# One decoder layer on one core: the first head's loads, the end of the out-projection and the block ring's places are rearranged

## The chip, the cores and the metric

One core of a Trainium2 chip runs the whole layer in one launch. The metric is the device time in microseconds. A few executions of a kernel are timed and the median is given; one more execution is recorded by the hardware profiler, and its page and trace are what the rows below come from.

## What is computed

Batch 1, 512 tokens behind 16 learned meta tokens (528 positions), width 2048, one layer, everything in fp32:

```python
h = concatenate([meta, x])                       # 528 x 2048
p = rmsnorm(h, g_mix) @ w_in                     # 2048 x 6144: q, k, v, b, c, u of 1024 columns each
o_attn = stick_breaking_attention(rmsnorm(q), rmsnorm(k), v)    # 8 heads of 128
o_conv = b * causal_dwconv3(c * u)                              # 1024 channels
h = h + concatenate([rmsnorm(o_attn), rmsnorm(o_conv)]) @ w_out
n2 = rmsnorm(h, g_ffn)
h = h + (silu(n2 @ w_gate) * (n2 @ w_up)) @ w_down              # 5632 inner columns
return h[16:]
```

Nearly all the work is in the products with w_in, w_out, w_gate, w_up and w_down.

## The kernel before

Activations lie transposed: 16 tiles of 128 channels by 528 (later 512) positions. Each fp32 operand is used as a sum of two parts, hi (rounded to the format fp32r) and lo (what is left), and a product is three matmuls: hi·hi, hi·lo, lo·hi.

**The weight stream.** All weights come in one fixed order, the list `loads`, on SyncE's DMA queue (SP) into four places of `w_buf`, each 128 partitions by 1024 columns. For each weight, ScalarE (ACT) casts it into hi (L189) and VectorE (DVE) subtracts to get lo (L190), into one of three slots of `s_buf`. `next_w` keeps two to three splits ahead of TensorE (PE), and when a place has been used for the last time, `done_with` issues the next load into it, so a load waits for VectorE's split. Every engine runs its instructions in the order in which they were put down; a scheduler sets that order when the program is built, with priorities, and it does not change at run time.

**Pairs.** The conv group (from its third channel tile on), the FFN's gate and up products (44 pairs) and the down product use products of 2x2 blocks in seven block products instead of eight: `pair_product` takes the blocks in the order 0 to 6 (the first pair of a kind begins with block 5), and VectorE adds weight quadrants for it (L198, L215). The blocks of the activations are formed once, stored in DRAM, and loaded again.

**Stages.** First head (k and q products side by side while x arrives, then v and the attention), seven more heads, the conv group, the out-projection (w_out), the FFN's 44 pairs, the down product. The places that the change and the prediction touch:

- *The first head* (L362 to L388). For each of five groups of k tiles (2, 2, 4, 4, 4): load x tiles (`load_x`, L341, also on SyncE), cast nh (L348 on ScalarE, L350 on GpSimd for the odd tiles from the fourth on), nl on VectorE (L351), one step of the k and of the q product, squares (L356, L359) and their adds (L360). The names in the trace: pk, pq, pv are the three products' accumulators, ssx the sum of squares over all channels (L330), which gives x's norm. Small vectors (gains) come in `vec` (L72).
- *The out-projection's end* (L887 to L970, called "the seam" in the prediction). For 16 output tiles, the attention half (acts `oa`) and the conv half (acts `oc`) of the product go to two halves of an accumulator `po`. The residual then takes four VectorE or GpSimd steps (L902 to L905), a scaling, and splits into the FFN's blocks f. Blocks 3, 4 and 6 go through DRAM (`fx`), since there is no room for them until the out-projection's buffers are released: the six loads f<-fx (L952, on GpSimd's queue) stand behind the last tile. `h_scale` is the norm of the FFN's input, a chain of small operations on all positions.
- *The ring* (L1028 to L1103). The down product takes its 22 k tiles in chunks of 4, 6, 6 and 6. Each chunk needs seven blocks of activations, loaded from DRAM (ring<-fd, L1042, on GpSimd's queue) into twelve ring places; chunk 0's blocks 1 to 6 lie in buffers of their own, `first`, and its block 0 in ring place 0. Places 1, 3, 4, 5 share memory with `first` and open when chunk 0 is done. `out_T<-d` (L1071) are the stores that add results to the output.

```python
    groups = {0: (0, 1), 1: (1, 2), 3: (1, 1), 4: (1, 1), 5: (1, 1), 6: (2, 1), 7: (2, 5)}
    def ring_place():
        n_ring[0] += 1
        return ring[(n_ring[0] - 1) % 12]
```

In `groups`, `i: (p, m)` says that m places from number i on lie in buffer p.

Of the kernel before, what the change touches and what calls it, by code (L numbers as in the profile page):

```python
# [15 lines left out]
P = 128  # L16
D = 2048
# [16 lines left out]
def hybrid_layer(ctx: ExitStack, tc: tile.TileContext, xT, w_in, w_out, w_gu, w_down, vecs, out):  # L34
# [37 lines left out]
    gp.dma_start(vec, vecs)  # L72
# [21 lines left out]
    carry = const.tile([P, P], F32R, name="carry")  # L94
    ve.tensor_copy(carry, later)
    ve.tensor_copy(carry[0:1, :], ones[0:1, :])
    ones_r = keep.tile([P, P], F32R, name="ones_r")
    ve.tensor_copy(ones_r, ones)
    later_r = const.tile([P, P], F32R, name="later_r")
    ve.tensor_copy(later_r, later)  # L100
# [44 lines left out]
    for i, b in ((0, 1), (1, 1), (0, 0), (1, 0), *((i, b) for i in range(2, KT) for b in range(2))):  # L145
        plan_raw(w_out[OUT_TILES[i], b], 8)
# [10 lines left out]

    quads, sums, split_w, used, loaded = {}, {}, [], [0], [0]
# [8 lines left out]

    def load_at(place):
        key, n, w = loads[loaded[0]]
        loaded[0] += 1  # L170
        t = w_buf[:, place : place + n * P]
        quads[key] = t, place, n
        nc.sync.dma_start(t.rearrange("p (t c) -> p t c", t=2) if len(w.shape) == 3 else t, w)

    def done_with(key):
        _, place, n = quads[key]
        if loaded[0] < len(loads):
# [126 lines left out]
    def square_sum(acc, src, first, s=None):  # L304
        if first:
            sc.activation(acc, src, AF.Square)
        else:
            s = t512(src.shape[-1], "r", 3)[:, : src.shape[-1]] if s is None else s
            sc.activation(s, src, AF.Square)
            gp.tensor_tensor(acc, acc, s, ALU.add)  # L310
# [32 lines left out]
    def split_x(k):  # L343
# [3 lines left out]
        if k < 4 or k % 2 == 0:  # L347
            sc.activation(nh, xts[k], AF.Copy, scale=g)  # L348
        else:
            gp.tensor_scalar(nh, xts[k], g, 0.0, ALU.mult, ALU.add)  # L350
# [17 lines left out]
    load_at(PLACES[0])  # L368
    load_x(0)
    load_at(PLACES[1])  # L370
    for a, b in FIRST:
        for k in range(len(xts), b):
            load_x(k)
        if not a:
            load_at(PLACES[2])
            load_at(PLACES[3])
        for k in range(a, b):
            split_x(k)
        if b == KT:
            for k in range(a, b):  # L380
                square_x(k)
            after(8, x_scale)
        for step in steps:
            next(step)
        if b < KT:
            for k in range(a, b):
                square_x(k)
# [86 lines left out]
    def head(h):  # L474
# [9 lines left out]
        after(8, qk_norm(halves(pk, H), g_k, L, kn[:, :L], (kh, kl, 384), f"k{h}"))  # L484
# [9 lines left out]
        after(9 if h else 10, qk_norm(pq[:, 0, :], gq_s, SEQ, qn, (qh, ql, SEQ), f"q{h}"))  # L494
# [125 lines left out]
    for h in range(HEADS):  # L620
        if h:
            after(6, lambda h=h: form_blocks(h - 1))
# [44 lines left out]
    for j in range(CONV_FIRST):  # L667
        if j == 0:
            after(2, lambda: form_blocks(7))
# [113 lines left out]
    for j in range(CONV_FIRST, HEADS, 2):  # L783
# [19 lines left out]
        for m in range(2):  # L803
            s = t512(SEQ, "e", 2)[:, :SEQ] if j == HEADS - 2 else cpool.tile([P, SEQ], F32, tag="s", name=f"sq{j}_{m}")
            conv_out(j + m, gbs[m][:, META - C0 :], ys[m], slots[m][:, 0], slots[m][:, 1], s, ve)
# [79 lines left out]
    for i in range(2):  # L885
        run(wide_product(ps_out[i][:, 0, :], oa))
    for i, j in enumerate(OUT_TILES):  # L887
        hj = wide_tmp("h", bufs=2)
        gp.dma_start(hj, xT[j][:, META:])
        if 0 < i < KT - 1:  # L890
            ps = new_ps()
            run(wide_product(ps[:, 0, :], oa))
            run(wide_product(ps[:, 1, :], oc))
        ps = ps_out[i]
        t1, t2 = wide_tmp("t1"), wide_tmp("t2")
        half, k = divmod(j, 8)
# [4 lines left out]
        def residual(eng):  # L901
            ve.tensor_tensor(t1, ps[:, 0, :], acc_a, ALU.mult)  # L902
            eng.tensor_tensor(hj, hj, t1, ALU.add)
# [16 lines left out]
        if i == KT - 1:  # L920
            with tc.high_priority(1 << 20):
                residual(ve)
                square_sum(acc_h, hj, False, wide_tmp("s"))
                mixed_blocks()
            oapool.release()
# [7 lines left out]
            rings, n_ring, ring = {}, [7], {}  # L933
# [16 lines left out]
            for s, n in ((3, 7), (4, 7), (6, 8)):  # L950
                for part in range(2):
                    gp.dma_start(acts[s][:, part, :n], fx[s][:, part, :n], max_dma_last_dim=4096)  # L952
            split_f(3, 6)
            split_f(4, 7)
        else:
# [244 lines left out]
```

## Time and profile before

| | us |
|---|---|
| median of 3 executions | 2069.37 (2069.09 to 2069.38) |
| the profiled execution | 2071.88 |
| its span on the core | 2069.7 |
| TensorE busy in the span | 2038.4 (98%) |
| VectorE / ScalarE / GpSimd busy | 1724.3 / 1046.4 / 412.3 |
| mean granted TensorE clock | 0.994 |

How to read the rows: a group row gives the busy time, the number of instructions and the mean length; a timeline row gives the start in the span, the length, the engine, the kernel's line, the operation, and in brackets how long the engine stood idle before and what released it. Rows of a wait list give the total, the number and the longest. The rows of stretches give the busy time of each engine in a window, then the TensorE clock that was granted (1.00 is full speed), the DMA engines' busy share and what they moved. SPq is SyncE's queue, PEld are TensorE's weight loads.

### The profile page before, as it was taken

How to read it: one execution, taken by the hardware profiler on the slowest of the kernel's cores; microseconds unless marked ns; L12 is line 12 of the kernel's file. 1: busy time of each engine (PE TensorE's matmuls, PEld its weight loads, DVE VectorE, ACT ScalarE, POOL GpSimd, SP SyncE). 2: the span in 40 equal slices, each digit the busy share in tenths (PEclk: the TensorE clock that was granted, in tenths of full speed). 3: DMA queues.
4: the chain of work that ended last, by engine and by line, in shares of the span. 5: the costliest groups of instructions: out<-in, count | busy, mean ns of one | idle time of the engine just before them, and what ended most of it. 6: DMA issues, size and time to landing. Idle time of an engine off the chain costs nothing.

```text
span 2069.7 us, 39728 instructions
## 1 busy us (share of the span) xinstructions
PE 2038.4 (98%) x16158; PEld 1972.2 (95%) x16158; DVE 1724.3 (83%) x2186; ACT 1046.4 (51%) x1511; POOL 412.3 (20%) x559
## 2 busy tenths in 40 slices
PE   7999999999999998999999999999999999999999
PEld 6999999999998887999999999999999999999999
DVE  7878877578877677898998998998999987888887
ACT  5666666444443434455555545555554543444443
POOL 4111111220014444111011011111111252223110
PEclk9999999999999999999999999999999999999999
DMA  6343334563356656556465565565555999989864
GB/s 207 106 152 123 113 123 136 206 172 103 102 195 192 186 169 222 159 160 184 148 173 159 148 173 148 151 172 158 155 167 158 284 308 266 252 241 248 238 155 87
DMA packets 161687, 362.21 MB, mean 175 GB/s; under 512 B 13457, under 2 KB 73361, under 8 KB 161505
## 3 DMA queue, kind: packets, MB, share of 16 engines
q1 hardware_dynamic: 78368, 225.80, 34.7%
q0 software_dynamic: 83136, 133.89, 24.5%
q8 instruction: 126, 2.06, 0.4%
q14 instruction: 57, 0.46, 0.1%
HBM read 278.76 MB, written 80.87 MB: 174 GB/s over the span
## 4 chain that ended last, share of the span: by engine, by line
PE 92%; DVE 3%; DMA 1%; ACT 1%; issue 1%; POOL 0%; SPq 0%; DVEq 0%; ACTq 0%; POOLq 0%
PE x L732 13%; PE x L734 13%; PE x L733 13%; PE z L732 6%; PE z L733 6%; PE z L734 6%; PE y L733 3%; PE y L732 3%; PE y L734 3%; PE po L831 3%; PE po L833 3%; PE po L832 3%; PE pv L276 1%; PE pv L278 1%; PE pv L280 1%; PE pk L278 1%
## 5 line engine op out<-in xcount | busy, mean ns | idle before, releaser
L189 ACT CAST s_buf<-w_buf 128x1024 fp32r<-128x1024 f32 (+2 forms) x665 | 659.5, 992 | 789.9 <-PE x L733 360.5
L190 DVE TENSOR_TENSOR s_buf<-w_buf,s_buf 128x1024 fp32r<-128x1024 f32 (+2 forms) x665 | 769.8, 1158 | 186.4 <-ACT s_buf L189 185.5
L734 PE MATMUL x<-f,s_buf 128*128 128x256 f32 x1408 | 388.8, 276 | 6.2 <-DVE s_buf L190 6.2
L733 PE MATMUL x<-f,s_buf 128*128 128x256 f32 x1408 | 388.6, 276 | 1.3 <-DVE f L291 1.3
L732 PE MATMUL x<-f,s_buf 128*128 128x256 f32 x1408 | 388.6, 276 | 0.2 <-ACT f L290 0.2
L198 DVE TENSOR_TENSOR w_buf<-w_buf 128x1024 f32<-128x1024 f32 (+1 forms) x243 | 278.6, 1146 | 18.9 <-DMA w_buf<-w_in 10.1
L734 PEld LDWEIGHTS x<-f,s_buf 128*128 128x128 f32 x1408 | 265.7, 189 | 6.4 <-DVE s_buf L190 6.4
L733 PEld LDWEIGHTS x<-f,s_buf 128*128 128x128 f32 x1408 | 265.6, 189 | 1.5 <-DVE f L291 1.5
L732 PEld LDWEIGHTS x<-f,s_buf 128*128 128x128 f32 x1408 | 265.7, 189 | 0.5 <-ACT f L290 0.4
L1004 POOL DMA_DIRECT2D fd<-s x147 | 103.7, 923 | 694.5 <-DVE s L291 692.9
L734 PE MATMUL z<-f,s_buf 128*128 128x256 f32 x704 | 193.6, 275 | 0.0
L733 PE MATMUL z<-f,s_buf 128*128 128x256 f32 x704 | 193.6, 275 | 0.0
L732 PE MATMUL z<-f,s_buf 128*128 128x256 f32 x704 | 193.6, 275 | 0.0
L732 PE MATMUL x<-ring,s_buf 128*128 128x256 f32 x608 | 168.5, 278 | 3.9 <-DVE d L1085 3.9
L734 PE MATMUL x<-ring,s_buf 128*128 128x256 f32 x608 | 168.3, 277 | 0.7 <-DVE s_buf L190 0.7
L733 PE MATMUL x<-ring,s_buf 128*128 128x256 f32 x608 | 168.3, 277 | 0.0
L733 PEld LDWEIGHTS z<-f,s_buf 128*128 128x128 f32 x704 | 132.2, 188 | 0.1
L732 PEld LDWEIGHTS z<-f,s_buf 128*128 128x128 f32 x704 | 132.2, 188 | 0.0
L734 PEld LDWEIGHTS z<-f,s_buf 128*128 128x128 f32 x704 | 132.2, 188 | 0.0
L1071 POOL DMA_DIRECT2D out_T<-d x62 | 59.5, 989 | 308.5 <-DVE d L1079 241.7
L732 PEld LDWEIGHTS x<-ring,s_buf 128*128 128x128 f32 x608 | 115.4, 190 | 4.1 <-DVE d L1085 4.1
L734 PEld LDWEIGHTS x<-ring,s_buf 128*128 128x128 f32 x608 | 115.3, 190 | 0.9 <-DVE s_buf L190 0.9
(380 smaller groups left out, 5285.8 us busy)
## 6 DMA issues: line engine op xcount, KB each, us to landing
w_buf<-w_gu SPq DMA_DIRECT2D x176, 512.0 KB, 3.5
w_buf<-w_in SPq DMA_DIRECT2D x92, 512.0 KB, 3.4
fd<-s POOLq DMA_DIRECT2D x147, 256.0 KB, 5.3
w_buf<-w_down SPq DMA_DIRECT2D x96, 384.0 KB, 4.9
ring<-fd POOLq DMA_DIRECT2D x42, 768.0 KB, 9.2
w_buf<-w_out SPq DMA_DIRECT2D x32, 512.0 KB, 3.4
out_T<-d POOLq DMA_DIRECT2D x62, 256.0 KB, 5.5
fc<-st SPq DMA_DIRECT2D x8, 1040.0 KB, 6.2
```

Of the source, the lines that this page charges most:

```text
L189: sc.copy(hi, src)
L190: ve.tensor_tensor(lo, src, hi.bitcast(F32), ALU.subtract)
L198: ve.tensor_tensor(sums[name], a, b, ALU.add)
L278: pe.matmul(ps, wh, al[:, a:b], start=False, stop=False)
L732: pe.matmul(p, hi[:, kk], act(0, k), start=start and j == k == 0, stop=False, skip_group_check=skip)
L733: pe.matmul(p, hi[:, kk], act(1, k), start=False, stop=False, skip_group_check=skip)
L734: pe.matmul(p, lo[:, kk], act(0, k), start=False, stop=k == n - 1, skip_group_check=skip)
L831: pe.matmul(ps, hi[:, kk], ah, start=k == order[0], stop=False)
L832: pe.matmul(ps, hi[:, kk], al, start=False, stop=False)
L833: pe.matmul(ps, lo[:, kk], ah, start=False, stop=k == order[-1])
L1004: gp.dma_start(fd[c][s][:, :, k], t[:, :, i])
L1071: gp.dma_start(two(out[j]), c, accum_op=ALU.add)
```

## The change

Three parts and a small one.

**A, the first head.** `vec` is loaded by SyncE ahead of everything. The first group's loads don't share four places: each of the ten head weights and v's first two get a place of their own in `w_buf` (`HEAD_PLACES`), and their end doesn't trigger a load (`EARLY`). All of these and the 16 x tiles are issued at the start. All x casts are on ScalarE and all adds of squares on VectorE, after the products; `x_scale` and the first head's norms are called two to three k tiles later. `form_blocks` (blocks of x for the conv group) is called one head later.

SyncE's queue at the start, before (xt are x tiles, w_buf weights; in brackets the semaphores that an instruction waits for, DMAHW of an earlier transfer, DVE of VectorE):

```order
L173 DMA w_buf<-w_in 128x256
L341 DMA xt_132<-xT 128x528
L173 DMA w_buf<-w_in 128x256
L341 DMA xt_135<-xT 128x528
L173 DMA w_buf<-w_in 128x256
L173 DMA w_buf<-w_in 128x512 [waits DMAHW0_49,DVE_49]
L173 DMA w_buf<-w_in 128x256
L341 DMA xt_179<-xT 128x528
L173 DMA w_buf<-w_in 128x512 [waits DMAHW2_49,DVE_49]
L341 DMA xt_181<-xT 128x528 [waits DMAHW1_49]
L173 DMA w_buf<-w_in 128x512 [waits DMAHW4_49,DVE_49]
```

and now:

```order
L72 DMA vec<-vecs 128x75
L172 DMA w_buf<-w_in 128x256
L340 DMA xt_127<-xT 128x528
L172 DMA w_buf<-w_in 128x256
L340 DMA xt_130<-xT 128x528
L172 DMA w_buf<-w_in 128x256
L340 DMA xt_133<-xT 128x528
L172 DMA w_buf<-w_in 128x256
L340 DMA xt_136<-xT 128x528 [waits DMAHW0_49]
L172 DMA w_buf<-w_in 128x512 [waits DMAHW1_49]
L340 DMA xt_139<-xT 128x528 [waits DMAHW2_49]
L340 DMA xt_141<-xT 128x528 [waits DMAHW3_49]
```

The waits for VectorE are gone from these rows; each transfer from the ninth on waits for the one eight before it.

**B, the out-projection's end.** The last two tiles go attention 14, attention 15, conv 14, conv 15 instead of tile by tile, and the attention half of the residual is a step of its own (`attention_half`). The last k tile of block 6 is split in place, so no block has more than seven k tiles to load from `fx`, and the loads come in the order 6, 3, 4. The last tiles' adds, `h_scale` (without its high priority) and the last tile's square add run on VectorE, and the last two output stores on SyncE.

GpSimd's queue there, before (f<-fx are the loads of blocks, acc_h and the work tiles belong to the norm):

```order
L970 DMA out_T<-w_7816 128x512
L310 TENSOR_TENSOR acc_h<-acc_h,w_7887 128x512
L961 DMA fx_6638<-st_7883 256x1x256
L952 DMA f_7929<-fx_6636 128x2x896 x2
L310 TENSOR_TENSOR acc_h<-acc_h,w_7900 128x512
L952 DMA f_7929<-fx_6637 128x2x896 x2
L952 DMA f_7930<-fx_6638 128x2x1024
L291 TENSOR_TENSOR work_r<-acc_h,work_r 128x512
L952 DMA f_7930<-fx_6638 128x2x1024
L299 TENSOR_TENSOR work_b<-work_a 128x512
```

and now:

```order
L985 DMA out_T<-w_7761 128x512
L309 TENSOR_TENSOR acc_h<-acc_h,w_7785 128x512
L892 DMA w_7822<-xT 128x512
L982 DMA fx_6636<-st_7780 256x1x256
L982 DMA fx_6637<-st_7780 256x1x256
L965 DMA f_7926<-fx_6638 128x2x896 x2
L965 DMA f_7925<-fx_6636 128x2x896 x2
L965 DMA f_7925<-fx_6637 128x2x896 x2
L1019 DMA fd_0_7952<-s_2_8205 256x1x256
```

The six loads stand in one row, with no operation of GpSimd between or behind them.

**C, the ring.** The ring starts at place 6 instead of 7, so that chunk 1 uses places 6 to 11 and then 0. Its sixth block is loaded with the fifth, in the last group of chunk 0, and its seventh in the middle of that group, as soon as place 0 (chunk 0's block 0) is free.

GpSimd's queue at the end of chunk 0, before (fd_5 and fd_6 are chunk 1's sixth and seventh block):

```order
L1042 DMA ring_17474<-fd_4_7965 128x2x768
L1042 DMA ring_7925<-fd_5_7966 128x2x768
L1071 DMA out_T<-d 256x1x256 x2
L1042 DMA ring_7925<-fd_5_7966 128x2x768
L1071 DMA out_T<-d_17446 256x1x256 x4
L1042 DMA ring_18326<-fd_6_7967 128x2x768 x2
L1071 DMA out_T<-d 128x512
```

and now:

```order
L1057 DMA ring_17472<-fd_4_7963 128x2x768
L1057 DMA ring_17472<-fd_5_7964 128x2x768
L1086 DMA out_T<-d 256x1x256 x2
L1057 DMA ring_17472<-fd_5_7964 128x2x768
L1057 DMA ring_7921<-fd_6_7965 128x2x768 x2
L1086 DMA out_T<-d_17444 256x1x256 x4
L1086 DMA out_T<-d 128x512
```

The seventh block's load has moved ahead of four output stores.

**D, the out-projection's start.** Its first two products go over the conv tiles in two parts; the parts are of four and four tiles instead of six and two. The last pair of conv outputs is put down at high priority.

The diff's core:

```diff
-    gp.dma_start(vec, vecs)
+    nc.sync.dma_start(vec, vecs)
...
+    EARLY = {loads[i][0]: i for i in range(2 * len(FIRST) + 2)}
+    HEAD_PLACES = [sum(2 * (b - a) * P for a, b in FIRST[:i]) + m * (b - a) * P for i, (a, b) in enumerate(FIRST) for m in range(2)]
+    HEAD_PLACES += [4096, 5120]
...
-        if loaded[0] < len(loads):
+        if key not in EARLY and loaded[0] < len(loads):
...
-        if k < 4 or k % 2 == 0:
-            sc.activation(nh, xts[k], AF.Copy, scale=g)
-        else:
-            gp.tensor_scalar(nh, xts[k], g, 0.0, ALU.mult, ALU.add)
+        sc.activation(nh, xts[k], AF.Copy, scale=g)
...
-            (gp, ve)[k % 2].tensor_tensor(accs[k % 2], accs[k % 2], s, ALU.add)
+            ve.tensor_tensor(accs[k % 2], accs[k % 2], s, ALU.add)
...
+    for i, (a, b) in enumerate(FIRST):
+        for m in range(2):
+            load_at(HEAD_PLACES[2 * i + m])
+            for k in range(len(xts), (a + b) // 2 if m == 0 else b):
+                load_x(k)
+    for place in HEAD_PLACES[2 * len(FIRST) :]:
+        load_at(place)
...
+            for place in PLACES:
+                load_at(place)
...
+    for k in range(KT):
+        square_x(k)
+    after(10, x_scale)
...
-        after(8, qk_norm(halves(pk, H), g_k, L, kn[:, :L], (kh, kl, 384), f"k{h}"))
+        after(8 if h else 11, qk_norm(halves(pk, H), g_k, L, kn[:, :L], (kh, kl, 384), f"k{h}"))
...
-        after(9 if h else 10, qk_norm(pq[:, 0, :], gq_s, SEQ, qn, (qh, ql, SEQ), f"q{h}"))
+        after(9 if h else 12, qk_norm(pq[:, 0, :], gq_s, SEQ, qn, (qh, ql, SEQ), f"q{h}"))
...
-        if h:
-            after(6, lambda h=h: form_blocks(h - 1))
+        if h > 1:
+            after(6, lambda h=h: form_blocks(h - 2))
...
-            for k in order[part * 6 : part * 6 + 6] if parts > 1 else order:
+            for k in order[part * 4 : part * 4 + 4] if parts > 1 else order:
...
+    def attention_half(i, eng):
+        hj, t1 = wide_tmp("h", bufs=2), wide_tmp("t1")
+        gp.dma_start(hj, xT[OUT_TILES[i]][:, META:])
+        ve.tensor_tensor(t1, ps_out[i][:, 0, :], acc_a, ALU.mult)
+        eng.tensor_tensor(hj, hj, t1, ALU.add)
+        return hj
...
+        elif i == KT - 2:
+            hs = [attention_half(m, ve) for m in (i, i + 1)]
+        if i >= KT - 2:
+            hj = hs[i - KT]
+            run(wide_product(ps_out[i][:, 1, :], oc))
...
-            for s, n in ((3, 7), (4, 7), (6, 8)):
+            for s in (6, 3, 4):
                 for part in range(2):
-                    gp.dma_start(acts[s][:, part, :n], fx[s][:, part, :n], max_dma_last_dim=4096)
+                    gp.dma_start(acts[s][:, part, :7], fx[s][:, part, :7], max_dma_last_dim=4096)
             split_f(3, 6)
             split_f(4, 7)
+            split_f(6, 3)
...
-            token_scale(acc_h, acc_h, D, "h", (w[:, 0], w[:, 1], a[:, 0], a[:, 1], b), gp)
+            token_scale(acc_h, acc_h, D, "h", (w[:, 0], w[:, 1], a[:, 0], a[:, 1], b))
...
-            rings, n_ring, ring = {}, [7], {}
+            rings, n_ring, ring = {}, [6], {}
...
-        for s in ((0, 1), (2, 3), (4,))[j - 1] if j else ():
+        for s in ((0, 1), (2, 3), (4, 5))[j - 1] if j else ():
...
+            (lambda: load_acts(1, 6)) if j == KT // 4 - 1 else None, lambda: second_sums(4 * j, c2, 2),
...
-            for s in (5, 6):
-                load_acts(1, s)
```

More of the change, by code (lines that the diff above doesn't have):

```diff
@@ L367, in hybrid_layer @@
     ]
-    load_at(PLACES[0])
-    load_x(0)
-    load_at(PLACES[1])
-    for a, b in FIRST:
[L372 to L376, printed above, removed]
+    for i, (a, b) in enumerate(FIRST):
[5 more added lines that the diff above has]
+        load_at(place)
+    limit[0] = 2 * len(FIRST)
+    for a, b in FIRST:
         for k in range(a, b):
@@ L379, in hybrid_layer @@
         if b == KT:
-            for k in range(a, b):
-                square_x(k)
-            after(8, x_scale)
+            for place in PLACES:
+                load_at(place)
+            limit[0] = len(ents)
         for step in steps:
             next(step)
-        if b < KT:
-            for k in range(a, b):
-                square_x(k)
+    for k in range(KT):
+        square_x(k)
+    after(10, x_scale)
+    later_r = const.tile([P, P], F32R, name="later_r")
+    ve.tensor_copy(later_r, later)
+    carry = const.tile([P, P], F32R, name="carry")
+    ve.tensor_copy(carry, later)
+    ve.tensor_copy(carry[0:1, :], ones[0:1, :])
     xpool.release()
@@ L968, in hybrid_layer @@
         if i < KT - 1:
-            square_sum(acc_h, hj, i == 0, wide_tmp("s"))
-        (gp if i < KT - 1 else nc.sync).dma_start(out[j], hj)
+            square_sum(acc_h, hj, i == 0, wide_tmp("s"), gp if i < KT - 2 else ve)
+        (gp if i < KT - 2 else nc.sync).dma_start(out[j], hj)
     assert not waiting
```

48 lines of the change are left out of this document (22 added, 26 removed).

## The prediction

> **What bounds the kernel now.** I read the page's head first (the engines' busy shares and the slices), then TensorE's list of waits, then busy time by stretch, and last the timelines around each place where TensorE stands still.
>
> ```profile
> span 2069.7 us, 39728 instructions
> PE 2038.4 (98%) x16158; PEld 1972.2 (95%) x16158; DVE 1724.3 (83%) x2186; ACT 1046.4 (51%) x1511; POOL 412.3 (20%) x559
> ```
>
> TensorE is busy for 2038.4 of 2069.7 us. The change removes no matmul, so what it can win is TensorE's 31.3 us of idle time and the time its matmuls lose at a lower clock. Stretches (us, busy time of PE, PEld, DVE, ACT, POOL, granted clock, DMA share, GB/s):
>
> ```profile
> 5.09:45.49 40.40, 30.43 (x149) 23.73 (x149) 32.83 (x40) 24.11 (x41) 18.91 (x14) 0.92 0.64 216
> 787.90:820.00 32.10, 24.40 (x179) 23.62 (x178) 23.57 (x29) 12.65 (x20) 13.49 (x12) 0.84 0.86 295
> 795.00:800.00 5.00, 4.94 (x43) 4.95 (x43) 4.97 (x9) 4.11 (x8) 1.83 (x3) 1.00 1.10 413
> 1000.00:1500.00 500.00, 500.00 (x4414) 500.00 (x4413) 450.93 (x499) 257.35 (x342) 67.69 (x96) 1.00 0.55 159
> 1690.00:1731.00 41.00, 37.71 (x331) 37.34 (x329) 38.26 (x51) 18.12 (x23) 15.57 (x18) 1.00 1.14 319
> 1731.00:1740.00 9.00, 8.08 (x46) 8.11 (x47) 1.78 (x4) 1.93 (x3) 1.37 (x3) 0.62 0.90 293
> 2030.00:2069.70 39.70, 35.52 (x314) 35.33 (x312) 29.13 (x44) 13.34 (x20) 3.44 (x4) 0.99 0.36 70
> ```
>
> The middle of the FFN is solid (500.00 of 500 busy). Idle time sits in the first head's k and q products (40.40 − 30.43 = 10.0), at the seam from out-projection to FFN (32.10 − 24.40 = 7.7), in the down product's first ring chunk, and in the tail (39.70 − 35.52 = 4.2), which the change leaves as it is. The clock is below 1.00 in the same places. TensorE's smaller waits (total, times, longest); the two big ones stand with their parts below:
>
> ```profile
> PE pk L278 <- DVE nl L351: 4.5, 8, 0.8
> ...
> PE x L733 <- DVE f L291: 1.3, 1, 1.3
> PE po L831 <- ACT oc_end L660: 1.2, 1, 1.2
> ...
> PE x L732 <- ACT f L290: 0.2, 1, 0.2
> ```
>
> **Part A: the head.** SyncE's own waits in the first 100 us; rows of TensorE, VectorE and ScalarE (start, length, engine, line, the wait before it in brackets); and from the page the groups of weight casts and splits (busy, mean ns):
>
> ```profile
> SPq L173 <- DVE s_buf L190: 48.7, 15, 8.1
> ```
> ```profile
> 25.25 0.41 PE L276 MATMUL pk<-nh,s_buf 128*128 128x264 f32 x2
> 25.50 0.40 PE L276 MATMUL pq<-nh,s_buf 128*128 128x512 f32 x1
> 25.73 0.40 PE L278 MATMUL pk<-nl,s_buf 128*128 128x264 f32 x2
> ...
> 36.22 0.51 PE L276 MATMUL pk<-nh,s_buf 128*128 128x264 f32 x2 [1.76 <-POOL nh L350]
> ...
> 38.73 0.64 PE L280 MATMUL pk<-nh,s_buf 128*128 128x264 f32 x2
> 39.17 0.64 PE L276 MATMUL pk<-nh,s_buf 128*128 128x264 f32 x2
> ...
> 43.54 1.05 PE L330 MATMUL ssx<-acc_x,ones 128*128 128x264 f32 x4
> 45.49 0.51 PE L276 MATMUL pv<-nh,s_buf 128*128 128x264 f32 x2 [0.89 <-ACT tmp L452]
> ```
> ```profile
> 5.07 0.77 DVE L351 SCALAR_TENSOR_TENSOR nl<-xt,vec,nh 128x528 fp32r<-128x528 f32 x1 [0.26 <-ACT nh L348]
> ...
> 16.43 2.92 DVE L351 SCALAR_TENSOR_TENSOR nl<-xt,vec,nh 128x528 fp32r<-128x528 f32 x2
> ```
> ```profile
> 5.84 0.74 ACT L348 ACTIVATE nh<-xt,vec 128x528 fp32r<-128x528 f32 x1
> ```
> ```profile
> L189 ACT CAST s_buf<-w_buf 128x1024 fp32r<-128x1024 f32 (+2 forms) x665 | 659.5, 992 | 789.9 <-PE x L733 360.5
> L190 DVE TENSOR_TENSOR s_buf<-w_buf,s_buf 128x1024 fp32r<-128x1024 f32 (+2 forms) x665 | 769.8, 1158 | 186.4 <-ACT s_buf L189 185.5
> ```
>
> The head's x tiles stand in SyncE's queue behind weight loads that wait for VectorE to free one of four places (48.7 us over 15 waits). So data come at 216 GB/s, where this chip moved 413 at 795 to 800. The change removes that wait: each head load gets a place of its own, and SyncE waits only for the transfer eight before it.
>
> What is next to bind? Per k tile there are three pk items (two matmuls each, 25.50 − 25.25 = 0.25 us) and three pq items (25.73 − 25.50 = 0.23): 1.43 us, and 16 tiles make 22.9 us. Data: 16 x tiles of 0.27 MB and 2.1 MB of weights are 6.4 MB; at 413 GB/s 15.5 us, at the old 216 GB/s 29.7. I take 350, between them and nearer the fast row (there too transfers were queued without a gap): 18.3 us from about 2, so the last x lands near 20.5. ScalarE now casts all x tiles: 16 by 0.74, and 4096 weight columns by 0.99 per 1024, are 16 us, so in 20 it keeps up; with a backlog of four x tiles its last cast is near 24. VectorE has 16 nl by 0.77 and 4 × 1.16 of splits, 17 us, and loses the slowdown beside GpSimd's casts (two nl in 2.92 at 16.43); its last nl is near 25. TensorE with 22.9 us from about 4.8 ends at 27.7 at the earliest; I add 1.3 for the last group, whose data come last: 29. pv can start at 29.3 where it started at 45.49; the ssx matmuls (1.05) now lie inside pv. That is 16.2 − 1.05 = 15.1 us. Behind it the squares' adds (14 of about 0.7 on VectorE, half of them GpSimd's before) run during pv, and x's scale and the norms come 2 to 3 k tiles later than before, so up to 1 us may show before the attention products: **14 us**. Bounds: data at 216 GB/s would end at 31.7, pv at about 35, and 10.5 − 1.05 leaves 9; a last group in time gives 16.
>
> **Part B: the seam.** TensorE's, VectorE's and GpSimd's rows and the chain's DMA step:
>
> ```profile
> 813.61 0.58 PE L734 MATMUL x<-f,s_buf 128*128 128x256 f32 x1 [6.22 <-DVE s_buf L190]
> 813.99 0.41 PE L732 MATMUL x<-f,s_buf 128*128 128x256 f32 x1
> 814.21 0.41 PE L733 MATMUL x<-f,s_buf 128*128 128x256 f32 x1
> ...
> 819.75 0.30 PE L732 MATMUL x<-f,s_buf 128*128 128x256 f32 x1
> ```
> ```profile
> 788.35 1.45 POOL L952 DMA_DIRECT2D f<-fx  x2 [0.68 <-PE po L833]
> ...
> 802.80 0.72 POOL L952 DMA_DIRECT2D f<-fx  x1
> ...
> 810.37 2.10 POOL L302 TENSOR_TENSOR acc_h<-work_a,work_b 128x512 f32<-128x512 f32 x1
> ```
> ```profile
> 810.08 1.27 DVE L198 TENSOR_TENSOR w_buf<-w_buf 128x1024 f32<-128x1024 f32 x1 [4.30 <-DMA w_buf<-w_gu]
> 811.28 2.28 DVE L190 TENSOR_TENSOR s_buf<-w_buf,s_buf 128x1024 fp32r<-128x1024 f32 x1
> ```
> ```profile
> 799.90 10.09 DMA w_buf<-w_gu
> ```
>
> The chain is: six f<-fx loads (four of 0.92 and two of 1.05 MB, 5.8 together) are issued from 788.35 to 802.80, between GpSimd's own adds, and fill the DMA engines; a w_gu load among them takes 10.09 us; VectorE stands in order behind it for 4.30, then runs at half speed beside GpSimd's adds (2.28 for a split, against a mean of 1.16); TensorE waits 6.22. After it the matmuls come 0.21 apart until 819.75, where the FFN's middle has 500 / 4414 = 0.113: 27 of them by 0.1 is 2.7, and the first is 0.27 slow too. With the short waits for f (0.2 and 1.3 us) the seam loses 10.6.
>
> After the change two of the six loads may go before the last tile is done, the rest right at its end in one row, all six of 0.92 now, so that 3.7 MB are left behind the seam's start: at 413 GB/s 9 us. The w_gu load, issued 12 us after the seam's start before and some 10.5 now, then finds the engines free, lands about 4 us later and is split by 17, ahead of its use at 18 (807.4 − 787.9, less the 1.5 of waits that go). The attention half of the last tiles' residual is done early, two of four VectorE operations fewer at the end and one weight split (1.16) less among them, so f comes about 2 us sooner, and the waits of 0.2 and 1.3 go. New there: five h_scale operations of about 0.7 and the last tile's adds move from GpSimd to VectorE, about 4 us in a stretch where VectorE has 23.57 of 32.10 busy. VectorE is then the late one: I count two short waits of TensorE for the second pair's first block, about one cast (0.99) and one split (1.16). Left are 2 to 4 us, gained **7**. Bounds: 9.5 if nothing waits, 4.5 if a half-speed stretch of 2.8 and another us of waiting follow the new waits.
>
> Does it? The wait of 1.76 at 36.22 was followed by spacings of 0.44 (38.73 to 39.17), the wait of 1.3 in the seam by none (795 to 800 has clock 1.00). The Trainium skill, TensorE: Matmul & The Clock Gate, Part 1, says the clock halves only after an idle window of about 3.4 us. By that page the new waits cost nothing more and the seam would gain 10.6 − 2.2 = 8.4. The row of 1.76 us speaks against it as a hard rule; the sum stays at 7.
>
> The out-projection's start waited 1.2 us for a late conv block. It now takes four tiles first, then four, so the late ones are asked for later by two k tiles of two products (2 × 2 × 3 × 0.23 = 2.8 us): **1**, between 0 and 1.5.
>
> **Part C: the ring.**
>
> ```profile
> 1731.92 0.77 PE L732 MATMUL x<-ring,s_buf 128*128 128x256 f32 x2 [3.93 <-DVE d L1085]
> ```
> ```profile
> 1722.37 2.01 POOL L1042 DMA_DIRECT2D ring<-fd  x2
> ```
> ```profile
> ring<-fd POOLq DMA_DIRECT2D x42, 768.0 KB, 9.2
> ```
>
> The row names VectorE's d, but d was long done: the block loaded at 1722.37 (a median load takes 9.2) lands at about 1731.6. It is chunk 1's seventh block, whose old place opened only when chunk 0's buffers were released. Its new place is that of chunk 0's first block, free when the first of the last group's seven blocks is done, and its load stands ahead of that group's out_T rows on GpSimd. That removes 3.93 and the slow matmuls behind (clock 0.62 from 1731 to 1740, 8.08 us busy, so up to 8.08 × 0.38 = 3.1): 7.0. The loads come into a full stretch (share 1.14, 319 GB/s), so a w_down weight may be later: **6**, between 0 and 7.
>
> **Sum.** 14 + 7 + 1 + 6 = 28. The profiled execution took 2071.88 us around a span of 2069.7, 2.5 above the median of 2069.37, so it would become 2043.9 and the median 2041.4. A measurement of this kernel tells 0.2% (4 us) from no change.
>
> **Rivals.** *1, the head gives half.* Data come at the old pace, or short waits keep the clock at half, at which the 96 items take 0.44 each, 42 us. For: waits of this size did it twice in the old head. Against: they came from a starved queue, and TensorE will have more work than it gets data late. Half speed throughout would take all of part A and 3 more (2058); half of it leaves A at 5 to 9 and the time at 2046 to 2050. Chance 0.13, likeliest about 2049.
>
> *2, a stall moves instead of going.* At the seam VectorE's backlog, or in the ring a weight load late behind two more block loads, gives back 5 to 9 of B's and C's 13. For: DMA share 1.14 there, VectorE 4.97 of 5.00 busy at 795 to 800. Time 2046 to 2050, chance 0.14.
>
> *3, VectorE becomes the bound of the FFN.* It is busy 450.93 of 500, 17.2 us in each pair of 7 × 24 matmuls (19.1 at 0.113). If the buffers' new addresses or the backlog slowed it by over 1.9 us a pair (11%), every one of the 44 pairs would pay; from 2.6 us on, (2.6 − 1.9) × 44 = 31 us outweigh the gain of 28, and the kernel is slower, 2073 or more. For: it has been at half speed beside GpSimd (811.28). Against: the loop's own operations are unchanged and GpSimd only issues transfers there. Chance 0.04.
>
> *4, the change does not do what it says*: the rule of eight outstanding transfers paces the head as before and the seam's late load stays late: 2066 to 2072. SyncE's waits name VectorE, not a transfer, so 0.03.
>
> **Numbers.** Forecast 0.66, rivals 0.13, 0.14, 0.04, 0.03. Faster by over 0.2%: 0.66 + 0.13 + 0.14 = 0.93; same 0.03; slower 0.04. High end of the gains: 16 + 9.5 + 1.5 + 7 = 34, time 2035.4. The range 2036 to 2053 takes in the forecast, rival 2 and most of rival 1.
>
> **What would show it.** Right: pv starts near 29 to 30 with 350 GB/s or more until 21; no wait over 1.5 us at the seam and six f<-fx issues in one row; the ring's first blocks of chunk 1 without a wait and clock 1.00 there. Wrong: spacings of 0.44 in the head; TensorE waiting for L190 after the seam by over 3 us; a w_down load over 12 us near 1700; TensorE below 500 of 500 in the FFN.

## The result and the profile after

| | before | changed |
|---|---|---|
| median of four executions, us | 2069.23 | 2048.96 (2047.93 to 2050.44) |
| ratio, 95% interval | 1 | 0.9897 (0.9885 to 0.9909) |
| the profiled execution / its span | 2071.88 / 2069.7 | 2050.44 / 2048.7 |
| TensorE busy | 2038.4 | 2032.3 |
| mean granted clock | 0.994 | 0.998 |

The change gains 20.3 us. 28 were forecast, so the time lies in the range, in its upper part. Which term is missing shows when the starts of the same matmuls are set side by side (us; read from the matmuls' rows in the two traces):

| matmul | before | changed | gained so far | forecast so far |
|---|---|---|---|---|
| first pv of head 0 | 45.49 | 31.75 | 13.7 | 16.2 |
| first of the out-projection (po) | 611.62 | 598.51 | 13.1 | 14 |
| first of the FFN (y<-f) | 787.89 | 775.14 | 12.7 | 15 |
| last of the FFN (x<-f) | 1637.75 | 1623.66 | 14.1 | 22 |
| last of the down product (x<-ring) | 2065.25 | 2044.28 | 21.0 | 28 |

The head and the ring did what was forecast. The seam, from the out-projection's end into the FFN, gave 1.4 us where 7 were expected. The page's head and the stretches of the changed kernel (busy time of PE, PEld, DVE, ACT, POOL, clock, DMA share, GB/s):

```profile
span 2048.7 us, 39716 instructions
PE 2032.3 (99%) x16158; PEld 1969.3 (96%) x16158; DVE 1719.6 (84%) x2202; ACT 1049.3 (51%) x1517; POOL 381.7 (19%) x535
```
```profile
5.09:30.00 24.91, 24.27 (x142) 21.47 (x141) 21.89 (x34) 22.74 (x40) 0.00 (x0) 1.00 1.02 379
...
760.00:800.00 40.00, 34.24 (x221) 30.38 (x220) 32.93 (x49) 17.30 (x28) 6.12 (x9) 0.98 0.75 250
800.00:830.00 30.00, 29.49 (x237) 29.29 (x237) 24.27 (x27) 14.31 (x20) 1.40 (x2) 0.91 0.34 107
...
1000.00:1500.00 500.00, 500.00 (x4414) 500.00 (x4413) 450.46 (x500) 258.35 (x344) 64.94 (x93) 1.00 0.54 159
...
1710.00:1740.00 30.00, 30.00 (x267) 30.00 (x267) 25.63 (x37) 14.15 (x21) 7.51 (x10) 1.00 1.03 275
```

In the head the DMA engines move 379 GB/s (216 before) and TensorE is busy 24.27 of 24.91. In the ring's stretch it is busy 30.00 of 30 at full clock. At the seam 5.8 us of idle time are left between 760 and 800, and the clock is at 0.91 behind them. TensorE's rows there, then VectorE's, GpSimd's, and the DMA step from the chain of waits:

```profile
790.24 0.38 PE L734 MATMUL x<-f,s_buf 128*128 128x256 f32 x1 [0.67 <-ACT s_buf L188]
791.55 0.39 PE L735 MATMUL x<-f,s_buf 128*128 128x256 f32 x1 [0.81 <-DMA f<-fx]
796.31 0.39 PE L736 MATMUL x<-f,s_buf 128*128 128x256 f32 x1 [1.83 <-DVE s_buf L189]
799.29 0.58 PE L734 MATMUL x<-f,s_buf 128*128 128x256 f32 x1 [2.13 <-DVE u L770]
```
```profile
791.45 1.23 DVE L197 TENSOR_TENSOR w_buf<-w_buf 128x1024 f32<-128x1024 f32 x1 [1.84 <-DMA w_buf<-w_gu]
...
793.89 1.23 DVE L197 TENSOR_TENSOR w_buf<-w_buf 128x1024 f32<-128x1024 f32 x1 [0.88 <-DMA w_buf<-w_gu]
...
798.21 0.69 DVE L298 TENSOR_TENSOR work_b<-work_a 128x512 f32<-128x512 f32 x1 [1.36 <-ACT work_a L297]
798.82 0.42 DVE L770 SCALAR_TENSOR_TENSOR u<-x,sides 128x256 f32<-128x256 f32 x1
```
```profile
775.62 2.87 POOL L965 DMA_DIRECT2D f<-fx  x4 [5.62 <-PE po L836]
```
```profile
785.42 8.38 DMA w_buf<-w_gu
```

This is the old chain in a new place. Four f<-fx loads go out within 2.87 us, and the w_gu load issued 10 us later still takes 8.38 from issue to landing (10.09 before, 3.5 in the median of all w_gu loads of before). VectorE waits for two of them, 1.84 and 0.88, and its own splits come late. Now a third thing stands in the same queue: h_scale's L298 waits 1.36 for ScalarE, and u (L770), which the next product needs, stands behind it. One f<-fx load is itself late (0.81). TensorE's four waits are 5.4 us where 7.7 were, and a half-speed stretch follows as before: 27 matmuls in a row near 0.213 us apart (799.7 to 805.4) where 0.113 is the spacing of the FFN's middle, 2.7 us too long.

### The profile page after: what moved, and what is told of

It is laid out like the page before. It is cut to its first block, busy times and chain, and to the rows that moved or that the text cites. A ratio compares the mean times of both kernels' runs of the same rounds, so it can differ in the third digit from the quotient of the medians.

```text
span 2048.7 us, 39716 instructions
## 1 busy us (share of the span) xinstructions
PE 2032.3 (99%) x16158; PEld 1969.3 (96%) x16158; DVE 1719.6 (84%) x2202; ACT 1049.3 (51%) x1517; POOL 381.7 (19%) x535
## 4 chain that ended last, share of the span: by engine, by line
PE 91%; DVE 4%; ACT 2%; issue 1%; DMA 1%; POOL 0%; SPq 0%; DVEq 0%; ACTq 0%; POOLq 0%
PE x L734 13%; PE x L736 13%; PE x L735 13%; PE z L734 6%; PE z L735 6%; PE z L736 6%; PE y L734 3%; PE y L735 3%; PE y L736 3%; PE po L834 3%; PE po L835 3%; PE po L836 3%; PE pv L275 1%; PE pv L277 1%; PE pv L279 1%
```

## The experiments

All ratios are to the kernel before, timed beside each run on the same chip. FFN stage is the time from the first y<-f to the last x<-f matmul in the profiled execution: 849.9 before, 848.5 in the changed kernel.

| run | median, us | ratio, 95% interval | FFN stage |
|---|---|---|---|
| e1_head_only | 2054.57 | 0.9918 (0.9904 to 0.9933) | 846.6 |
| e2_seam_only | 2069.42 | 0.9999 (0.9989 to 1.0008) | 845.9 |
| e3_ring_only | 2062.90 | 0.9965 (0.9952 to 0.9978) | 848.5 |
| e4_hscale_gpsimd | 2045.70 | 0.9882 (0.9866 to 0.9899) | 843.6 |
| e5_changed_again | 2048.85 | 0.9899 (0.9883 to 0.9916) | 847.9 |
| e6_late_f4 | 2047.06 | 0.9892 (0.9878 to 0.9907) | 845.9 |
| e7_hscale_gpsimd_row | 2046.87 | 0.9893 (0.9878 to 0.9908) | 845.4 |
| e8_vec_gpsimd | 2046.52 | 0.9893 (0.9878 to 0.9908) | 845.9 |
| e9_no_f4_loads | 2041.83 | 0.9859 (0.9845 to 0.9872) | 840.1 |
| e10_gpsimd_casts | 2059.80 | 0.9946 (0.9934 to 0.9959) | 847.8 |
| e11_casts_only | 2062.43 | 0.9962 (0.9949 to 0.9976) | 847.5 |
| e12_best | 2047.53 | 0.9885 (0.9870 to 0.9901) | 845.2 |

**Each part alone.** First the parts, put into the kernel before one at a time: A (the first head's loads, casts and adds), B (the out-projection's end), C (the ring). The short forms of the three edits:

```diff
+    HEAD_PLACES = [...]          # e1: all of part A
...
+            for s in (6, 3, 4):   # e2: all of part B
...
-            rings, n_ring, ring = {}, [7], {}
+            rings, n_ring, ring = {}, [6], {}   # e3: all of part C
```

> The kernel before with part A (the first head) alone. Theory (parts add up, as the two traces' marks suggest: the out-projection's first matmul comes 13.1 us earlier in the changed kernel): 13 to 14 us less than before, about 2055.5, with the first pv matmul near 31.8. Rival (the head's gain needs the other parts, or part D gives some of it): under 10 us. If the prediction's own price of 14 was right for the wrong reason, pv would start near 29.3 instead.

> The kernel before with part B (the end of the out-projection) alone. Theory (the waits there are not removed but replaced: the marks gain only 1.4 us across this stretch in the changed kernel): 1 to 2.5 us less than before, about 2067.5, with four waits of TensorE between the out-projection's end and the second pair and slow matmuls behind them. Rival (the prediction's 7 is there, and something that parts A or D moved eats it in the changed kernel): 5 to 7 us less, about 2063.

> The kernel before with part C (the ring's places) alone. Theory (the late seventh block was the whole of that wait, its slow matmuls too): 6.5 to 7 us less than before, about 2062.4, no wait above 1 us between 1700 and 1745, clock 1.00 there. Rival (the two earlier block loads make a w_down load late in the full stretch): 0 to 4 us less, with a wait of TensorE for a split (L190) before 1730.

Measured, against 2070.16 for the kernel before beside them: 15.6 less, 0.7 less (not distinguishable from none) and 7.3 less. The sum, 23.6, is some 3 above the whole change's 20 to 21, and the parts stand in the order that the marks gave. The excess may be chance: of what e1's profile gains, 3.3 lie in the FFN stage (846.6 against 849.9), which part A doesn't touch. Head: pv starts at 30.51 and the out-projection's first matmul comes 13.7 sooner. Ring: the wait and the slow clock are both gone, as these stretches show (e3, in place of 37.71 and 8.08 busy, and clock 0.62):

```profile
1690.00:1731.00 41.00, 40.73 (x359) 40.56 (x358) 38.28 (x51) 18.93 (x24) 17.31 (x20) 1.00 1.15 322
1731.00:1740.00 9.00, 9.00 (x82) 9.00 (x81) 6.82 (x10) 4.62 (x8) 1.41 (x2) 1.00 1.10 329
```

The DMA share is as full as it was (1.15), and no weight came late by it. For the seam the rival's 5 to 7 us are excluded. The theory's waits are there (0.67, 2.69, 0.99 and 0.52 in e2's trace, with 16 matmuls in a row near 0.213 apart behind the second), and of its 1 to 2.5 us all but the last 0.2 lie inside the interval, as no gain does too. One more thing shows: the stage varies from one execution to the next. The kernels with the old seam have 849.9, 846.6 (e1), 848.5 (e3) and 847.5 (e11), mean 848.1; those with the new one 848.5, 847.9 (e5), 845.9 (e2), 845.9 (e8) and 847.8 (e10), mean 847.2. The profile of one execution can't tell less than 2 us here, and 0.9 between these averages isn't told from nothing.

**h_scale back on GpSimd.**

```diff
-        if True:
-            token_scale(acc_h, acc_h, D, "h", (w[:, 0], w[:, 1], a[:, 0], a[:, 1], b))
+        with tc.high_priority(1 << 20):
+            token_scale(acc_h, acc_h, D, "h", (w[:, 0], w[:, 1], a[:, 0], a[:, 1], b), gp)
```

> The changed kernel with h_scale back on GpSimd at high priority, as before. Theory (a late w_gu load, 8.38 us beside the six block loads, is what holds VectorE at the seam, and h_scale on VectorE only adds the wait of 2.13 behind it): the waits of 1.84 and 0.88 for w_gu stay, the wait of 2.13 goes, VectorE's splits beside GpSimd's adds get slower: 0 to 2 us less than the changed kernel, 2047 to 2049. Rival (VectorE's load by h_scale is the cause): TensorE's waits of 1.83 and 2.13 and the slow matmuls behind go together, 5 to 6.5 us less, about 2043.

2045.70, about 3 below the changed kernel by the ratios: between the two expectations, and its profile shows why neither fits. The first operation of h_scale on GpSimd waits for ScalarE, and the scheduler had put the sixth f<-fx load behind it. GpSimd's rows, the chain's two DMA pieces, and the landing of the w_gu load issued at 784.65 (least, median and most of this one load):

```profile
774.84 2.15 POOL L965 DMA_DIRECT2D f<-fx  x3 [5.58 <-PE po L836]
784.59 3.31 POOL L290 TENSOR_TENSOR work_r<-acc_h,work_r 128x512 fp32r<-128x512 f32 x1 [7.60 <-ACT work_r L289]
787.85 0.74 POOL L965 DMA_DIRECT2D f<-fx  x1
```
```profile
784.65 3.20 DMA w_buf<-w_gu
787.85 5.17 DMA f<-fx
```
```profile
DMA to landing us min/median/max: 5.9/5.9/5.9
```

The chain's first piece ends where the sixth load is issued, so its 3.20 is not what the w_gu load took: that load landed 5.9 us after its issue. (The expectation of e6 below takes this 3.20 for the load's time.) With one load of 0.92 MB held back until 787.85, the three w_gu loads of the seam took 4.7, 4.8 and 5.9 us instead of 8.2, 8.3 and 8.4, and VectorE had no wait for them. The waits of 1.83 and 2.13 are gone, but others came: TensorE waits 0.76 for h_scale's own sums, 1.37 for ScalarE and 1.33 for the load that was held back. Two things differ from the changed kernel: where h_scale runs, and when the sixth load goes out. The next two versions take them apart, with the changed kernel beside them.

**The two apart.** e6 leaves h_scale on VectorE and holds the sixth load back; e7 puts h_scale on GpSimd behind all six loads.

```diff
-                for part in range(2):
+                for part in range(2 if s != 4 else 1):          # e6
...
+        gp.tensor_scalar(acts[4][:, 1, 0, :2], sides[:, T2 : T2 + 2], 1.0, 0.0, ALU.mult, ALU.add)
+        gp.dma_start(acts[4][:, 1, :7], fx[4][:, 1, :7], max_dma_last_dim=4096)
...
-            token_scale(acc_h, acc_h, D, "h", (w[:, 0], w[:, 1], a[:, 0], a[:, 1], b))
+            token_scale(acc_h, acc_h, D, "h", (w[:, 0], w[:, 1], a[:, 0], a[:, 1], b), gp)   # e7
```

> The changed kernel itself, once more beside the next three, to compare them with on one chip. 20 to 22 us less than before, ratio 0.989 to 0.990. The profile tells how far the waits at the seam differ from one execution to the next: four to five waits, some 5 us together, and 20 to 30 slow matmuls.

> The changed kernel with h_scale on VectorE as it is, but with the last of the six f<-fx loads held back until ScalarE's second copy of the first FFN pair (some 10 us into the seam). Theory (what helped with h_scale on GpSimd was that the sixth load came to stand behind a waiting GpSimd operation, so the w_gu load took 3.20 instead of 8.38 us): w_gu near 3 to 5 us here too, VectorE's wait for it under 0.5, 2.5 to 4 us less than the changed kernel. Rival (h_scale's place was what helped): no gain, 0 to 1 us, with the wait for VectorE's u at 2 still there.

> The changed kernel with h_scale on GpSimd, but with the six f<-fx loads in one row ahead of it (no high priority). Theory (the loads' crowding is the cause): w_gu takes 8 us again and VectorE waits for it, so the time is that of the changed kernel within 1 us. Rival (h_scale's place): 2.5 to 4 us less than the changed kernel, as with h_scale on GpSimd at high priority.

Both come out about 2 below the changed kernel's 2048.85, and the intervals of all three overlap, so the times alone decide nothing. The traces do. e6: the w_gu loads take 4.7, 5.0 and 6.1 and VectorE's wait for them is down to 0.4, but now the load that was held back is the late one, 6.65 us after its issue, and TensorE waits 3.93 for it (TensorE, then the chain's step):

```profile
793.36 0.55 PE L735 MATMUL x<-f,s_buf 128*128 128x256 f32 x1 [3.93 <-DMA f<-fx]
```
```profile
786.57 6.65 DMA f<-fx
```

e7: w_gu takes 8.53 and VectorE's wait is back; without h_scale's operations in VectorE's queue the wait for u is gone, that for the split is not:

```profile
790.23 0.39 PE L735 MATMUL x<-f,s_buf 128*128 128x256 f32 x1 [0.83 <-DMA f<-fx]
794.87 0.38 PE L736 MATMUL x<-f,s_buf 128*128 128x256 f32 x1 [1.76 <-DVE s_buf L189]
```
```profile
783.84 8.53 DMA w_buf<-w_gu
```

So both causes are there: the loads' crowding, and h_scale's waits in VectorE's queue. Holding a load back chooses which transfer is late: with h_scale on GpSimd, TensorE's waits of over 0.5 sum to 4.0 both with the six loads in a row (e7) and with the sixth held back (e4). That points to the bytes themselves. Between 774 and 790 the DMA engines move 402 GB/s in e5, which is 6.4 MB in 16 us, at a rate that the best stretches shown here exceed by 3 to 4% (413 to 417):

```profile
774.00:790.00 16.00, 15.17 (x127) 14.54 (x125) 14.22 (x22) 10.72 (x18) 2.87 (x4) 1.00 1.11 402
```

**Fewer bytes.** If the bytes are the limit, taking some away must do what moving them did not. e9 leaves out block 4's two loads and reads block 3 in its place.

```diff
-            for s in (6, 3, 4):
+            for s in (6, 3):
...
-    acts_of = [act_of(acts[s]) for s in range(7)]
+    acts_of = [act_of(acts[s if s != 4 else 3]) for s in range(7)]
```

> The changed kernel without the two loads of block 4: the FFN's fifth block product reads block 3 in its place (that part of the computation is left out, every matmul is still there), and 1.8 of the 3.7 MB behind the seam's start are not moved. Theory (bytes within 15 us are the limit, since holding one load back only made that load the late one): w_gu lands in 4 to 5 us, no wait for f<-fx, no wait of over 0.5 for w_gu, no slow matmuls; the FFN stage (848 in two profiles of the changed kernel) is 842 to 843, 4 to 6 us less, about 2044. Rival (VectorE's and ScalarE's own order holds the seam): the waits for VectorE's u and for s_buf stay, 0 to 2 us less.

2041.83, and an FFN stage of 840.1, about 8 less than the changed kernel's and more than the 4 to 6 expected. 44 pairs of 168 matmuls by the 0.113 of the FFN's middle are 837.3, so of the 11 us that the stage lost in the changed kernel some 3 are left without these 1.8 MB. h_scale is still on VectorE. The stretch beside the one above, and TensorE's one wait left:

```profile
774.00:790.00 16.00, 16.00 (x139) 15.89 (x138) 15.72 (x24) 10.70 (x18) 1.44 (x2) 1.00 0.90 305
790.00:805.00 15.00, 13.56 (x118) 13.32 (x117) 13.66 (x17) 8.79 (x12) 0.00 (x0) 1.00 0.33 107
```
```profile
792.74 0.39 PE L736 MATMUL x<-f,s_buf 128*128 128x256 f32 x1 [1.44 <-DVE s_buf L189]
```

VectorE's wait for w_gu is 0.3, there is no wait for u, and the clock stays at 1.00. The rival (VectorE's and ScalarE's order holds the seam) falls: with the loads gone, h_scale's L298 on VectorE doesn't wait for ScalarE at all, and of the waits only one of 1.44 is left.

Two limits. The w_gu loads took 3.3, 4.4 and 5.95 (the last one no less than in e4 and e6), and with block 4's loads no product waits for block 4 any more; e9 can't tell the fewer bytes from that wait. And 402 GB/s is not what every execution had: the same stretch of e8, below, whose fourth f<-fx load takes 15.7 us, moves 348.

**The head's two halves.** The prediction put the head's gain down to the loads that no longer wait. e10 keeps those loads and gives GpSimd its six casts and half of the adds back; e11 keeps the old loads and only takes the casts and adds from GpSimd.

```diff
+        if k < 4 or k % 2 == 0:                     # e10, taken out of before in e11
+            sc.activation(nh, xts[k], AF.Copy, scale=g)
+        else:
+            gp.tensor_scalar(nh, xts[k], g, 0.0, ALU.mult, ALU.add)
```

> The changed kernel with GpSimd's casts of six x tiles and its half of the squares' adds back, the loads still without a wait. Theory (the loads were the bound, but VectorE is now 88% busy in the head and runs at half speed beside GpSimd): pv starts 3 to 5 us later than at 30 to 31.8, the time is 3 to 5 us above the changed kernel, about 2052. Rival (the loads alone made the gain): within 1 us of the changed kernel.

> The kernel before with only this: x casts on ScalarE and the adds of squares on VectorE, the loads behind the splits as before. Theory (data come at 216 GB/s, so casts gain only the wait of 1.76 for GpSimd and the slow matmuls behind it): 1 to 3 us less than before, pv at 43 to 45. Rival (GpSimd's slowing of VectorE held the splits and so the loads): 6 us or more less, pv at 39 or earlier.

Neither expectation was right in size. e10 is 2059.80, by the ratios some 10 above the changed kernel (3 to 5 were expected), with pv at 39.52; e11 is 7.6 below the kernel before (1 to 3 were expected), with pv at 38.60. At pv the loads alone are worth 6.0 us, the casts alone 6.9, and both together 13.7 to 15.5 in the profiles with part A whole: each alone gives nearly half, and the two nearly add up (12.9), as two costs on one path do. Three stretches of e10, then VectorE's and GpSimd's rows at one place in it:

```profile
15.00:20.00 5.00, 3.82 (x13) 2.53 (x13) 5.00 (x6) 3.46 (x6) 4.75 (x4) 0.74 1.05 400
20.00:25.00 5.00, 4.45 (x27) 4.03 (x28) 5.00 (x7) 1.95 (x4) 3.62 (x3) 0.92 1.03 409
...
30.00:35.00 5.00, 3.15 (x21) 2.68 (x19) 5.00 (x5) 2.10 (x4) 3.93 (x4) 1.00 0.19 50
```
```profile
18.87 2.94 DVE L350 SCALAR_TENSOR_TENSOR nl<-xt,vec,nh 128x528 fp32r<-128x528 f32 x2
```
```profile
18.36 1.16 POOL L349 TENSOR_SCALAR nh<-xt,vec 128x528 fp32r<-128x528 f32 x1
19.77 1.47 POOL L359 TENSOR_TENSOR acc_x<-acc_x,tmp 128x528 f32<-128x528 f32 x1 [0.25 <-ACT tmp L358]
```

The data come at 400 GB/s and are through soon after 25, but VectorE is busy 5.00 of 5.00 in every stretch from 15 to 35, with two operations in 2.94 us beside GpSimd's where one alone takes 0.77. In e11 it is the other way round: GpSimd does nothing, and between 10 and 35 the transfers run at 236 to 314 GB/s, SyncE waiting 23.5 us for splits in the first 50.

**The vec load and the best version.** e8 gives vec back to GpSimd's queue; e12 has that and e4's h_scale together.

```diff
-    nc.sync.dma_start(vec, vecs)
+    gp.dma_start(vec, vecs)
```

> The changed kernel with the vec load back on GpSimd, so that SyncE issues the first weight and the first x tile 0.45 us sooner. Theory (the first k product starts late, 6.42, and behind TensorE's pause at half speed, for x0 came late): the first pk at or before 5.3 and no half-speed matmuls behind, 1.5 to 2.5 us less than the changed kernel. Rival (x0 is paced by the transfers around it, or vec on GpSimd lands late and nh waits for it): within 0.7 us of the changed kernel.

> The changed kernel with h_scale on GpSimd at high priority (the sixth f<-fx load then stands behind a waiting GpSimd operation) and the vec load on GpSimd. Theory (the two gains of the earlier runs add, 3 and 1): 2044 to 2046, ratio to before 0.987 to 0.9885. Rival (both differences were within what executions differ by): 2047 to 2049.

e8's first pk starts at 5.78; with vec on SyncE it starts at 6.42, 5.61, 5.80 and 5.54 in four profiles. The theory (5.3 or earlier) falls. The 2.3 us below e5 are inside the intervals, so no gain is shown, and its profile has 2.0 of them in the FFN stage. The edit reaches that stage all the same, by a way that was not expected. GpSimd's rows there in e8, then its stretch:

```profile
765.11 1.71 POOL L965 DMA_DIRECT2D f<-fx  x2
774.47 2.86 POOL L965 DMA_DIRECT2D f<-fx  x4 [7.64 <-PE po L836]
```
```profile
774.00:790.00 16.00, 14.93 (x126) 14.35 (x124) 15.38 (x24) 10.69 (x18) 2.86 (x4) 1.00 1.00 348
```

The first two f<-fx loads go out 8.9 us before the FFN's first matmul; in the seven profiles that have part B and vec on SyncE it is 6.8 to 6.9, in the other two with part B and vec on GpSimd (e2, e12) 8.9 again. With the seam's code as in the changed kernel the stage is 848.5, 847.9 and 847.8 with vec on SyncE (changed kernel, e5, e10) and 845.9 twice with vec on GpSimd (e2, e8). So some of what looks like chance there may be this; how the vec load moves the seam's transfers stays open.

e12's 2047.53 lies in the rival's range and its ratio at the edge of the theory's; its interval overlaps those of e4 and of the changed kernel, so e4's 3 us stay unconfirmed. No version here that computes the whole layer is shown to be faster than the changed kernel.

## Why the prediction was right, and where not

The time is in the range because the range took in rival 2, at 2046 to 2050; the sum itself, 2041.4, was 7.6 too low. Of its four terms the ring's was right and the head's came near; of the out-projection's start nothing came and of the seam's 7 only 1.4. So the hit is owed to the width of the range, not to the sum.

- **Head, 14: right in sum, half right in its reason.** Measured 13.1 to 14.7 at the out-projection's start in eight profiles with part A whole (12.0 in e12, where a split in the conv group came 1.3 late), and 15.6 by the times of e1. The chain of steps was nearly right: pv near 30 to 31.8 (29.3 forecast), data at 379 GB/s (350). But that the "x tiles stand in SyncE's queue behind weight loads that wait" was only half of it. VectorE's half speed beside GpSimd, named as a side gain, was the other half (e10, e11). One step of the working was off: the squares are not all behind the products. Eleven of ScalarE's rows for them (L352, L355) lie among the casts before 27, so ScalarE is busy 22.74 of 24.91 and its last cast ends at 26.6, not 24.
- **A part of it is given back.** Between the last pv matmul of the eighth head and its last attention product the gain falls from 14.1 to 13.1. e1, e4 and e10 lose the same 1.0 to 1.1 there, e2, e3 and e11, without part A's calls, nothing. Of these calls `form_blocks`, which comes one head later, runs in that stretch; it was not tried alone.
- **Out-projection's start, 1: not there.** The wait of 1.24 for a conv block is gone, and one of 0.91 stands in its place, for the conv norm's first cast (ss_c). In the last two tiles' new order there is a wait of 0.33 for ScalarE's cast of st (L289). From start to end the out-projection is 0.4 us longer.
- **Seam, 7: the step that failed.** The w_gu load "then finds the engines free, lands about 4 us later": it took 8.38, because the four loads left behind the seam's start were counted alone (3.7 MB, 9 us), while four w_gu loads, two output stores and the end of an earlier f<-fx load share the same 16 us. 6.4 MB at 402 GB/s fill them (e5). The transfers' start was moved, their sum was not. The fewer f<-fx loads stand ahead, the sooner w_gu lands (8.1 to 8.3 with four in e5, 4.7 to 6.1 with three in e6, 3.3 to 5.95 with two in e9), so the crowding is shown; that the sum of bytes is the bound is the reading that fits e6 and e9, and is not shown by itself. The "two short waits" came out as four, 5.4 us. Rival 2 (a stall moves instead of going) is what happened, 5.6 us of it.
- **The short waits and the clock.** A half-speed stretch that costs 2.7 us does follow the new waits, so the bound of 4.5, not the 7, was the end to start from. The upper bound of 9.5 for no wait at all leaves out 1.1 of the 10.6 without a reason. The 8.4 that went by an idle window of 3.4 us was further off.
- **Ring, 6: right,** 6.9 by the marks, 7.3 by the times of e3. The wait named by VectorE's d was a DMA, though not for the reason given: a d (L1085) did end just ahead of the product, at 1731.81, but in e3 the same product starts at 1727.16, 4.4 us before that d, so it doesn't wait for it. The feared late weight did not come.
- **FFN, rival 3:** VectorE is busy 450.46 of 500, as before. Nothing of it.

## What to carry to other kernels

At a stage's edge, sum all bytes that must land before the next stage's first use, from every queue, against the rate that the trace has shown, before asking in which order they go: here the order mostly chose which transfer was late. Where an engine's wait and another engine's slowness sit on the same path, test them one at a time before giving one the credit: here each alone brought nearly half (6.0 and 6.9 of 13.7 to 15.5). A chain of small operations that waits for another engine can hold up whatever stands behind it in the queue: here h_scale's 1.36 on VectorE stood ahead of TensorE's 2.13.

## What the runs showed of the hardware that was not expected

TensorE's clock fell to half without any long pause, and the same waits did not always bring it down. At the changed kernel's seam the longest wait is 2.13 us, in e5 too, yet 27 and 22 matmuls in a row near 0.213 us apart follow four waits that sum to 5.4 us within 10. One wait of 3.93 (e6) was followed by 24, one of 1.44 (e9) by none. But e4 and e12 have the same waits at the seam to 0.06 us; here are TensorE's rows and a stretch behind them, first of e4, then of e12:

```profile
787.95 0.50 PE L635 MATMUL ss_h<-work_r,ones_r 128*128 128x512 f32 x1 [0.76 <-POOL work_r L290]
791.23 0.39 PE L734 MATMUL x<-f,s_buf 128*128 128x256 f32 x1 [1.37 <-ACT s_buf L188]
793.06 0.39 PE L735 MATMUL x<-f,s_buf 128*128 128x256 f32 x1 [1.33 <-DMA f<-fx]
793.00:798.00 5.00, 4.94 (x40) 4.80 (x41) 2.59 (x3) 1.05 (x1) 4.15 (x4) 1.00 0.29 105
```
```profile
790.25 0.50 PE L635 MATMUL ss_h<-work_r,ones_r 128*128 128x512 f32 x1 [0.75 <-POOL work_r L290]
793.53 0.39 PE L734 MATMUL x<-f,s_buf 128*128 128x256 f32 x1 [1.39 <-ACT s_buf L188]
795.41 0.38 PE L735 MATMUL x<-f,s_buf 128*128 128x256 f32 x1 [1.38 <-DMA f<-fx]
795.00:800.00 5.00, 4.59 (x26) 4.59 (x27) 1.51 (x2) 0.17 (x1) 4.39 (x4) 0.66 0.31 105
```

Behind e4's the clock is 1.00 and no row of matmuls is slow; behind e12's it is 0.66, and 16 in a row are 0.213 apart. The kernel before and e3, whose seam has the same code, show it once more: both wait 0.22 and then 1.26 us for f, and the six microseconds behind run at clock 1.00 in one and 0.72 in the other (before, then e3):

```profile
795.30:801.30 6.00, 6.00 (x52) 5.86 (x52) 5.97 (x10) 4.18 (x8) 2.67 (x4) 1.00 1.12 415
796.00:802.00 6.00, 6.00 (x40) 6.00 (x40) 5.70 (x10) 3.93 (x8) 1.52 (x3) 0.72 1.12 417
```

So neither the longest wait nor the waits' sum settles it in these runs; what else does stays open. The price of one such stretch is 1.2 to 2.7 us (12 to 27 matmuls of 0.1 too much at the seams). The Trainium skill's rule (TensorE: Matmul & The Clock Gate, Part 1) is an idle window of about 3.4 us. It fits e6 and e9, but read as one unbroken pause it doesn't fit the rows of 2.13 in the changed kernel and of 1.26 in e3.

The same program's first microseconds differ: with the same instructions in the head, the first x tile let the first product start between 5.5 and 6.4 us, and pv between 30.0 and 31.8. The latest of both is the changed kernel's profile, where the first four q products take 0.62 to 0.63 us each, until 10; in e5 they take 0.39 to 0.50.
